# Scores of the second mixer's attention: two heads per token tile, the low K part in 64 rows each

## The chip, the cores and the metric

The kernel runs on one core of a Trainium2 chip, as one program launched once. The metric is the device time of that program in microseconds (us); the number that counts is the median of several runs.

## The reference, cut to what matters

Two layers are applied to two request groups of 512 tokens with the same weights. The change touches the second layer's mixer only: an attention with 16 heads of width 64 and rotary positions.

```python
def odd_mixer(x, w_in, w_out):
    q, k, v = jnp.split(x @ w_in, 3, axis=-1)
    q = rope(to_heads(q, DA_HEADS)) * DA_HEAD_DIM ** -0.5
    k = rope(to_heads(k, DA_HEADS))
    v = to_heads(v, DA_HEADS)
    res = [dilated_branch(q, k, v, w, d) for (w, d) in DA_BRANCHES]
    wts = jax.nn.softmax(jnp.stack([r[1] for r in res]), axis=0)
    o = jnp.einsum('gbht,gbhtd->bhtd', wts, jnp.stack([r[0] for r in res]).astype(jnp.float32))
    return from_heads(o.astype(x.dtype)) @ w_out
```

The three branches, mixed by their softmax denominators, are the same as one softmax over all 512 keys of the score plus the logarithm of the number of branches that hold the pair of positions. The kernel computes it in that form: `logc` holds minus that logarithm, and a huge number where no branch holds the pair.

## The kernel before

**Stages.** Layer 0 has its mixer and its mixture of experts, layer 1 the same; the attention of the second mixer runs from about 1405 to 1880 us of the profiled span. Each stage hands its result to the next through memory.

**Precision.** Matrix products are made of parts: a value is split in a high part, which the fast matmul format holds exactly, and the low rest. A product is hi x hi + lo x hi + hi x lo. Softmax weights and V are multiplied in full 32-bit, which the profile shows as two matmul records for each matmul.

**A unit.** `odd` works through 16 units, one for each pair of heads `p` (0 to 7) and request group `g`. `da_unit` returns the slots of a unit, and `weave` runs the slots with the steps of the next unit's projections (`steps_t`, and `steps_n` for V) spread between them. A unit has 8 blocks: head `e` of the pair (0 or 1) by token tile `t` (0 to 3), 128 queries each against 512 keys.

**A block.** `q_stack` puts Q hi of a head in its own 64 rows (rows 0 to 63 for head 0, 64 to 127 for head 1) and Q lo in the other 64. `k_stack` puts K hi in both halves of a tile `a`, and K lo in the head's own half of a tile `b`; `zero_halves` has filled the other half of `b` with zeros once. So one matmul of 128 rows, `q` by `a`, gives Q hi x K hi + Q lo x K hi, and a second one, `q` by `b`, adds Q hi x K lo. Both write the PSUM tile `s` (two buffers). VectorE then adds `logc` and takes the minimum in one pass (L825), ScalarE takes the exponential with its sum (L827), and VectorE takes the reciprocal and scales the row (L828, L829).

**Turning and closing.** `turn` transposes a block's weights in four 128x128 matmuls against `ident` (L837) into a PSUM tile `t` (two buffers), and one copy by ScalarE or VectorE takes it to `pt`. The transposes of a block follow the scores of the block two places later, as `attend` keeps two waiting. `close` multiplies the weights by V: eight matmuls, alternately for head 0 and head 1, each of 64 weight columns, so that the two heads stand in the two column halves of TensorE. The page shows these as `o<-pt,v 128*64`.

**Order.** Each engine executes its list in order. The list is made at build time by a scheduler, which may move instructions between slots where data allow it; several matmuls of `close` are thus put between the next unit's scores. All matmuls go through the helper at L134, so the tile names (`acc` projections, `s` scores, `t` transposes, `o` weights by V) tell them apart. K lo lies in spare parts of boxes named `mraw` and `mrawb`: `s<-mraw,qk` and `s<-mrawb,qk` are the K lo matmuls, `s<-qk` those with K hi. In the trace `128*128` is rows by weight columns of the array that a matmul takes.

Of the kernel before, what the change touches and what calls it, by code (L numbers as in the profile page):

```python
# [12 lines left out]
F32 = mybir.dt.float32  # L13
# [3 lines left out]
AF = mybir.ActivationFunctionType  # L17
OP = mybir.AluOpType
# [3 lines left out]
G, T, D = 2, 512, 1024  # L22
KT = D // 128
NT = T // 128
# [98 lines left out]
class Trunk:  # L123
# [207 lines left out]
    def turn(self, keep):  # L331
        while len(self.turns) > keep:
            turn, i, close = self.turns.popleft()
            turn(i)
            if close:
                self.late.append(close)
# [110 lines left out]
    def na_unit(self, g, p, qk, V, biases):  # L447
# [3 lines left out]
        def block(i):  # L451
            e, c2 = divmod(i, 2)
            q, (kh, kl), bias = qk["q"][e], qk["k"][e], biases[e]
            hv, lv = (x.rearrange("p (r c) -> p r c", c=64) for x in (kh, kl))
            S = self.ps.tile([128, 2, 256], F32, name="s", bufs=2)
            P = PS[i] = pb.tile([128, 2, 256], F32, name="p", bufs=3)
            st = pb.tile([128, 4, 2], F32, name="sm_st", bufs=4)
            for j in range(2):
                cb = 2 * c2 + j
                qs = q[:, 128 * cb:128 * cb + 128]  # L460
                b = slice(BAND[cb], BAND[cb] + 32)
                self.mm(S[:, j], qs, hv[:, :, b], True, False)
                self.mm(S[:, j], qs, lv[:, :, b], False, True)
            for j in range(2):
                nc.vector.tensor_tensor_reduce(P[:, j], S[:, j], bias[:, VAR[2 * c2 + j]], 1.0, 0.0,
                                               OP.add, OP.max, st[:, 0, j:j + 1])
            nc.vector.tensor_scalar(st[:, 1], st[:, 0], -1.0, None, op0=OP.mult)
            for j in range(2):
                nc.scalar.activation(P[:, j], P[:, j], AF.Exp, bias=st[:, 1, j:j + 1],
                                     accum_out=st[:, 2, j:j + 1])  # L470
            nc.vector.reciprocal(st[:, 3], st[:, 2])
            for j in range(2):
                nc.vector.tensor_scalar(P[:, j], P[:, j], st[:, 3, j:j + 1], None, op0=OP.mult)

# [60 lines left out]
    def ml_unit(self, g, h, qk, md, cols, V):  # L535
# [14 lines left out]
        def score(s):  # L550
            (qh, ql), (kh, kl), nm, nd = qk["q"], qk["k"], u["nm"], u["nd"]
            S = self.ps.tile([128, T], F32, name="s", bufs=2)
            c = slice(s * 128, (s + 1) * 128)
            self.mm(S, kh[:, c], qh, True, False)
            self.mm(S, kh[:, c], ql, False, False)
# [256 lines left out]
    def da_unit(self, g, p, qk, V):  # L812
        nc, pb = self.nc, self.pb
        PT, PS = [None, None], {}

        def block(i):
            e, t = divmod(i, 4)
            q, (kh, kl) = qk["q"][e], qk["k"][e]
            S = self.ps.tile([128, T], F32, name="s", bufs=2)
            c = slice(t * 128, (t + 1) * 128)  # L820
            self.mm(S, q[:, c], kh, True, False)
            self.mm(S, q[:, c], kl, False, True)
            P = PS[i] = pb.tile([128, T], F32, name="p", bufs=3)
            st = pb.tile([128, 3], F32, name="sm_st", bufs=4)
            nc.vector.tensor_tensor_reduce(P, S, self.logc[:, 384 - t * 128:384 - t * 128 + T], 1.0, 0.0,  # L825
                                           OP.add, OP.min, st[:, 0:1])
            nc.scalar.activation(P, P, AF.Exp, bias=st[:, 0:1], scale=-1.0, accum_out=st[:, 1:2])  # L827
            nc.vector.reciprocal(st[:, 2:3], st[:, 1:2])  # L828
            nc.vector.tensor_scalar(P, P, st[:, 2:3], None, op0=OP.mult)  # L829

        def turn(i):
            e, t = divmod(i, 4)
            if t == 0:
                PT[e] = pb.tile([128, 4, T], F32, name="pt", bufs=self.pt_bufs)
            tp = self.ps.tile([128, 4, 128], F32, name="t", bufs=2)
            for k in range(NT):
                nc.tensor.transpose(tp[:, k], PS[i][:, k * 128:(k + 1) * 128], self.ident)  # L837
            self.copy_any(PT[e][:, :, t * 128:(t + 1) * 128], tp)

        def close():  # L840
            o = self.ps.tile([128, T], F32, name="o", bufs=1)
            hc = (p % 2) * 128
            for k in range(NT):
                for e in range(2):
                    self.mm(o[64 * e:64 * e + 64], V[g, p // 2][:, k, hc + 64 * e:hc + 64 * e + 64], PT[e][:, k],
                            k == 0, k == NT - 1)
            self.y_store(g, p, o)

        return self.attend(block, turn, close, 8)

    def odd(self):
        nc, pb, a = self.nc, self.pb, self.a
# [43 lines left out]
        after = self.loaded, self.normed  # L896
        with self.tc.issue_after(after[0]), self.tc.issue_after(after[1]):
            self.W["q0"] += self.subhalf(a["wo"][1], 1)
        self.zero_halves()
        lnf, ap = [pb.tile([128, D], F32, name="v4", bufs=4) for _ in range(2)], a["lnf"][0]  # L900
        for i, t in enumerate(lnf):
            nc.sync.dma_start(t, bass.AP(tensor=ap.tensor, offset=ap.offset + i * D, ap=[[0, 128], [1, D]]))
# [51 lines left out]
        for i, (p, g) in enumerate(acts):  # L954
# [3 lines left out]
            else:  # L958
                self.open_out(1)
                rest = self.out_steps(1, 0)  # L960
                fill = rest[:8]
            self.weave(slots, fill)
        self.weave([partial(self.turn, 1), partial(self.turn, 0), self.drain], rest[8:])

    def router_weights(self, layer):
        nc, pd = self.nc, self.pd
# [524 lines left out]
```

## Time and profile before

| | |
|---|---|
| median of three runs | 2823.64 us (2819.38 to 2824.97) |
| profiled execution, its own time | 2821.07 us |
| its span, first to last instruction | 2819.3 us |
| mean granted TensorE clock | 0.978 of full speed |
| PE busy (matmul) | 2690.2 us, 95% |
| PEld busy (weight load, beside PE) | 2251.3 us, 80% |
| DVE (VectorE) / ACT (ScalarE) busy | 2254.6 us, 80% / 1836.7 us, 65% |

Busy time of PE counts matmul records, which overlap their neighbours, as results drain while the next matmul streams. What one matmul costs is therefore read from the distance between two starts, not from its length.

### The profile page before, as it was taken

How to read it: one execution, taken by the hardware profiler on the slowest of the kernel's cores; microseconds unless marked ns; L12 is line 12 of the kernel's file. 1: busy time of each engine (PE TensorE's matmuls, PEld its weight loads, DVE VectorE, ACT ScalarE, POOL GpSimd, SP SyncE). 2: the span in 40 equal slices, each digit the busy share in tenths (PEclk: the TensorE clock that was granted, in tenths of full speed). 3: DMA queues.
4: the chain of work that ended last, by engine and by line, in shares of the span. 5: the costliest groups of instructions: out<-in, count | busy, mean ns of one | idle time of the engine just before them, and what ended most of it. 6: DMA issues, size and time to landing. Idle time of an engine off the chain costs nothing.

```text
span 2819.3 us, 39964 instructions
## 1 busy us (share of the span) xinstructions
PE 2690.2 (95%) x14376; PEld 2251.3 (80%) x14376; DVE 2254.6 (80%) x3867; ACT 1836.7 (65%) x2737; POOL 180.6 (6%) x111
## 2 busy tenths in 40 slices
PE   8999999979999999999599999999799999999995
PEld 7888889868888888888477767679588888888873
DVE  4467687689989898989786776775899999999976
ACT  3555443367777878788466665752578778787864
POOL 0000000410000000000000000004100000000002
PEclk9999999989999999999799999999899999999997
DMA  6411236689899999995411010155898999999853
GB/s 209 152 62 55 77 106 221 226 355 391 352 409 368 393 416 361 415 392 184 142 68 38 29 50 24 56 191 223 347 389 352 408 368 392 418 359 417 352 228 138
DMA packets 118838, 714.33 MB, mean 253 GB/s; under 512 B 18509, under 2 KB 30285, under 8 KB 73311
## 3 DMA queue, kind: packets, MB, share of 16 engines
q1 hardware_dynamic: 108703, 671.40, 59.9%
q0 software_dynamic: 9936, 40.37, 5.1%
q8 instruction: 113, 1.85, 0.3%
q14 instruction: 86, 0.70, 0.1%
HBM read 657.16 MB, written 55.66 MB: 253 GB/s over the span
## 4 chain that ended last, share of the span: by engine, by line
PE 42%; DVE 5%; ACT 2%; DMA 2%; issue 1%; POOL 0%; SPq 0%; POOLq 0%; DVEq 0%; ACTq 0%
PE acc L134 18%; PE o L134 11%; PE s L134 10%; PE t L837 1%; PE t L147 1%; ACT rp L805 1%; DMA mrawp<-ws 1%; DVE rp L809 0%; DVE rp L807 0%; DVE rp L808 0%; DVE qk L408 0%; DVE p L825 0%; PE t L887 0%; ACT p L827 0%; DVE mrawb L144 0%
## 5 line engine op out<-in xcount | busy, mean ns | idle before, releaser
L144 DVE TENSOR_TENSOR mlo<-mraw,mhi 128x1024 fp32r<-128x1024 f32 (+1 forms) x486 | 527.6, 1139 | 41.0 <-ACT mhi L144 38.8
L144 ACT CAST mhi<-mraw 128x1024 fp32r<-128x1024 f32 (+1 forms) x486 | 450.3, 989 | 27.6 <-PE acc L134 12.8
L144 DVE TENSOR_TENSOR mlo<-mrawp,mhi 128x1024 fp32r<-128x1024 f32 (+1 forms) x282 | 316.7, 1173 | 29.0 <-ACT mhi L144 27.6
L144 DVE TENSOR_TENSOR mlo<-mrawb,mhi 128x1024 fp32r<-128x1024 f32 (+1 forms) x264 | 295.2, 1169 | 19.6 <-ACT mhi L144 18.2
L134 PE MATMUL s<-mhi,xeh 128*128 128x512 f32 (+1 forms) x768 | 290.2, 378 | 0.0
L134 PE MATMUL acc<-mhi,xeh 128*128 128x512 f32 (+1 forms) x768 | 288.1, 375 | 1.9 <-ACT mhi L144 1.9
L134 PE MATMUL acc<-mlo,xeh 128*128 128x512 f32 (+1 forms) x768 | 287.6, 374 | 1.2 <-DVE mlo L144 1.1
L144 ACT CAST mhi<-mrawp 128x1024 fp32r<-128x1024 f32 (+1 forms) x282 | 270.1, 1014 | 27.5 <-POOL xres L1079 10.2
L134 PE MATMUL acc<-mhi,xel 128*128 128x512 f32 (+1 forms) x768 | 287.5, 374 | 0.0
L134 PE MATMUL s<-mlo,xeh 128*128 128x512 f32 (+1 forms) x768 | 285.3, 372 | 0.0
L134 PE MATMUL s<-mhi,xel 128*128 128x512 f32 (+1 forms) x768 | 285.3, 371 | 0.0
L134 PE MATMUL o<-mhi,hh 128*128 128x512 f32 x704 | 279.8, 397 | 0.0
L134 PE MATMUL o<-mhi,hl 128*128 128x512 f32 x704 | 275.6, 391 | 0.0
L134 PE MATMUL o<-mlo,hh 128*128 128x512 f32 x704 | 275.1, 391 | 0.0
L144 ACT CAST mhi<-mrawb 128x1024 fp32r<-128x1024 f32 (+1 forms) x264 | 251.1, 1013 | 11.5 <-PE acc L134 4.4
L134 PE MATMUL acc<-mrawb,mraw 128*128 128x256 f32 (+1 forms) x1416 | 217.5, 309 | 13.3 <-ACT mrawb L144 10.9
L134 PEld LDWEIGHTS acc<-mrawb,mraw 128*128 128x128 f32 x1416 | 194.4, 193 | 28.1 <-ACT mrawb L144 11.1
L134 PE MATMUL acc<-mraw,mrawb 128*128 128x512 f32 x792 | 203.5, 399 | 0.0
L134 PE MATMUL acc<-xh,mrawb 128*128 128x512 f32 x528 | 186.1, 406 | 0.0
L134 PEld LDWEIGHTS acc<-mraw,mrawb 128*128 128x128 f32 x792 | 144.0, 188 | 31.2 <-issue 3.2
L134 PEld LDWEIGHTS acc<-mhi,xeh 128*128 128x128 f32 x768 | 145.9, 190 | 24.8 <-ACT mhi L144 3.2
L134 PEld LDWEIGHTS acc<-mlo,xeh 128*128 128x128 f32 x768 | 145.8, 190 | 23.8 <-DVE mlo L144 2.6
(337 smaller groups left out, 5152.8 us busy)
## 6 DMA issues: line engine op xcount, KB each, us to landing
mraw<-ws SPq DMA_DIRECT2D x150, 1536.0 KB
mrawp<-ws SPq DMA_DIRECT2D x90, 1536.0 KB
mrawb<-ws SPq DMA_DIRECT2D x82, 1536.0 KB
mraws<-ws SPq DMA_DIRECT2D x26, 1536.0 KB
mraw<-wo SPq DMA_DIRECT2D x24, 512.0 KB
mraw<-we SPq DMA_DIRECT2D x16, 512.0 KB
yd<-yst SPq DMA_DIRECT2D x32, 256.0 KB
mraw<-wn SPq DMA_DIRECT2D x12, 512.0 KB
```

Source lines behind the costliest of these rows:

```text
L134: return self.nc.tensor.matmul(out, lhsT, rhs, start=start, stop=stop, skip_group_check=True)
L144: return [self.nc.scalar.copy(hi, src), self.nc.vector.tensor_tensor(lo, src, hi, op=OP.subtract)]
L147: out = f(*args, **kw)
L805: nc.scalar.copy(r[32 * i:32 * i + 32], ps[32 * j:32 * j + 32])
L837: nc.tensor.transpose(tp[:, k], PS[i][:, k * 128:(k + 1) * 128], self.ident)
```

## The change

`da_unit` no longer goes through `attend`. A slot is now a token tile `t` with both heads: the K hi matmuls of head 0 and head 1, then their K lo matmuls, each of which takes only the 64 rows in which the head's Q hi and K lo lie (rows 0 to 63, rows 64 to 127). Then the two softmax chains. `turn` transposes both heads' blocks of one token tile, and one token tile is kept waiting in place of two blocks. There are 4 slots in place of 8, with the same projection steps between them, twice as many to a slot. The `p` buffers are 4 in place of 3. `odd` no longer zeroes the other halves (`zero_halves` is left out there); layer 0 is as before.

```diff
-        def block(i):
-            e, t = divmod(i, 4)
-            q, (kh, kl) = qk["q"][e], qk["k"][e]
-            S = self.ps.tile([128, T], F32, name="s", bufs=2)
+        def pair(t):
             c = slice(t * 128, (t + 1) * 128)
-            self.mm(S, q[:, c], kh, True, False)
-            self.mm(S, q[:, c], kl, False, True)
...
+            S = [self.ps.tile([128, T], F32, name="s", bufs=2) for _ in range(2)]
+            for e in range(2):
+                self.mm(S[e], qk["q"][e][:, c], qk["k"][e][0], True, False)
+            for e in range(2):
+                u = slice(64 * e, 64 * e + 64)
+                self.mm(S[e], qk["q"][e][u, c], qk["k"][e][1][u], False, True)
+            for e in range(2):
+                P = PS[t, e] = pb.tile([128, T], F32, name="p", bufs=4)
...
+        def turn(t):
+            for e in range(2):
+                if t == 0:
+                    PT[e] = pb.tile([128, 4, T], F32, name="pt", bufs=self.pt_bufs)
+                tp = self.ps.tile([128, 4, 128], F32, name="t", bufs=2)
+                for k in range(NT):
+                    nc.tensor.transpose(tp[:, k], PS[t, e][:, k * 128:(k + 1) * 128], self.ident)
+                self.copy_any(PT[e][:, :, t * 128:(t + 1) * 128], tp)
...
-        return self.attend(block, turn, close, 8)
+        def slot(t):
+            pair(t)
+            if self.late:
+                self.late.popleft()()
+            self.turns.append((turn, t, close if t == NT - 1 else None))
+            self.turn(1)
+
+        return [partial(slot, t) for t in range(NT)]
...
-        self.zero_halves()
+        self.kl_next = [0, 0]
```

How the change moves instructions is seen in the built lists. First the start of a unit on PE (TensorE), before: `o` rows are the previous unit's weights by V, `s` rows the new unit's scores, each score tile with its K hi row and then its K lo row (the one with `mraw`).

```order
L134 MATMUL o_14458<-pt_14181,v4_13336 64x512
L134 MATMUL s_14406<-qk_14398,qk_14343 128x512
L134 MATMUL s_14406<-mraw_12722,qk_14343 128x512
L134 MATMUL s_14428<-qk_14398,qk_14343 128x512
L134 MATMUL s_14428<-mraw_12722,qk_14343 128x512
L134 MATMUL o_14458<-pt_14321,v4_13336 64x512
L134 MATMUL o_14458<-pt_14181,v4_13336 64x512
L134 MATMUL s_14449<-qk_14398,qk_14343 128x512
L134 MATMUL s_14449<-mraw_12722,qk_14343 128x512
L134 MATMUL o_14458<-pt_14321,v4_13336 64x512
```

All three blocks are of head 0. The same place on PE of the changed kernel, where `s_14402` and `s_14445` are head 0 and `s_14403` and `s_14446` head 1:

```order
L134 MATMUL s_14402<-qk_14394,qk_14354 128x512
L134 MATMUL s_14402<-mraw_12722,qk_14354 128x512
L134 MATMUL o_14463<-pt_14193,v4_13348 64x512
L134 MATMUL o_14463<-pt_14186,v4_13348 64x512
L134 MATMUL s_14403<-qk_14398,qk_14357 128x512
L134 MATMUL s_14403<-mraw_12722,qk_14357 128x512
L134 MATMUL s_14445<-qk_14394,qk_14354 128x512
L134 MATMUL s_14445<-mraw_12722,qk_14354 128x512
L134 MATMUL o_14463<-pt_14193,v4_13348 64x512
L134 MATMUL o_14463<-pt_14186,v4_13348 64x512
L134 MATMUL s_14446<-qk_14398,qk_14357 128x512
L134 MATMUL s_14446<-mraw_12722,qk_14357 128x512
```

Here the scheduler has pulled the two heads apart again: no K lo matmul stands beside the other head's, and each is a 64-row matmul between matmuls of 128 rows. The second place is on PE inside the same unit, before: two blocks with their transposes.

```order
L134 MATMUL s_14483<-qk_14398,qk_14343 128x512
L134 MATMUL s_14483<-mraw_12722,qk_14343 128x512
L837 MATMUL t_14492<-ident_60,p_14431 128x128 x4
...
L134 MATMUL s_14519<-qk_14402,qk_14346 128x512
L134 MATMUL s_14519<-mraw_12722,qk_14346 128x512
L837 MATMUL t_14528<-ident_60,p_14452 128x128 x4
```

And in the changed kernel, where both heads' scores and then both heads' transposes stand together:

```order
L134 MATMUL s_14516<-qk_14394,qk_14354 128x512
L134 MATMUL s_14517<-qk_14398,qk_14357 128x512
L134 MATMUL s_14516<-mraw_12722,qk_14354 128x512
L134 MATMUL s_14517<-mraw_12722,qk_14357 128x512
L839 MATMUL t_14534<-ident_60,p_14451 128x128 x4
L839 MATMUL t_14540<-ident_60,p_14457 128x128 x4
```

Counted over the whole PE list, the 128 K lo matmuls of the changed kernel stand as 30 neighbouring pairs and 68 single ones. Between matmuls of different array shape (128 by 128, 64 weight columns, 64 rows and the few others) there are 150 places before and 323 after. Of the difference, 98 lead into a 64-row stretch and 98 out of one (31 of these into `o`, 30 into transposes, 37 into other matmuls of full shape). The rest are 23 fewer: 27 fewer from `s` and `acc` into `o`, 5 fewer from `o` into transposes, 7 more from `o` into `s`, 2 more from `o` into `acc`. The deeper of the two column halves in each stretch of `o` matmuls, summed over all stretches, is 79 matmuls before and 77 after. VectorE has four MEMSETs fewer; no other engine has a computing instruction more or fewer.

## Rows read from the trace of the kernel before

**Rows 1.** Busy time of each engine in the attention and its middle part.

```profile
core 0: us, PE busy (x) PEld busy (x) DVE busy (x) ACT busy (x) POOL busy (x), PEclk, DMA share, GB/s
1412.00:1875.00 463.00, 453.96 (x2480) 336.21 (x2479) 346.06 (x808) 301.00 (x597) 0.00 (x0) 1.00 0.15 52
1500.00:1840.00 340.00, 333.54 (x1758) 240.91 (x1757) 243.87 (x575) 219.94 (x437) 0.00 (x0) 1.00 0.12 42
```

**Rows 2.** Waits in 1410:1875: weight loads (PEld), then matmuls (PE); total, times, longest.

```profile
PEld o L134 <- issue: 30.6, 97, 0.9
PEld s L134 <- DVE sm_st L825: 12.8, 17, 1.3
PEld s L134 <- ACT qk L419: 11.6, 13, 1.2
...
PE s L134 <- ACT qk L419: 5.4, 10, 0.8
PE t L837 <- DVE sm_st L828: 1.9, 9, 0.3
```

**Rows 3.** PE timeline at a unit's start: start, length, instruction, idle before.

```profile
1537.32 0.50 PE L134 MATMUL s<-qk 128*128 128x512 f32 x1 [0.27 <-ACT qk L419]
1537.65 0.40 PE L134 MATMUL s<-mraw,qk 128*128 128x512 f32 x1
1537.88 0.39 PE L134 MATMUL s<-qk 128*128 128x512 f32 x1
1538.12 0.40 PE L134 MATMUL s<-mraw,qk 128*128 128x512 f32 x1
1538.44 1.08 PE L134 MATMUL o<-pt,v 128*64 128x512 f32 x4
1539.45 0.50 PE L134 MATMUL s<-qk 128*128 128x512 f32 x1
1539.79 0.39 PE L134 MATMUL s<-mraw,qk 128*128 128x512 f32 x1
```

**Rows 4.** PE timeline inside a unit, scores, transposes, projection.

```profile
1548.76 0.40 PE L134 MATMUL s<-mraw,qk 128*128 128x512 f32 x1
1549.00 0.60 PE L837 MATMUL t<-ident,p 128*128 128x128 f32 x4
1549.35 0.48 PE L134 MATMUL acc<-xh,mrawb 128*128 128x512 f32 x1
1549.67 0.39 PE L134 MATMUL acc<-xl,mrawb 128*128 128x512 f32 x1
```

**Rows 5.** PE timeline, transposes that follow weights by V.

```profile
1687.55 1.93 PE L134 MATMUL o<-pt,v 128*64 128x512 f32 x6
1689.41 0.66 PE L837 MATMUL t<-ident,p 128*128 128x128 f32 x4
```

**Rows 6.** PE timeline in layer 0: eight transposes of 64 rows between projections.

```profile
267.04 1.29 PE L134 MATMUL acc<-mrawb,mraw 128*128 128x512 f32 x5
268.26 0.71 PE L530 MATMUL t<-ident,mw 64*128 64x64 f32 x8
268.90 0.74 PE L134 MATMUL acc<-mrawb,xh 128*128 128x512 f32 x2
269.48 0.40 PE L134 MATMUL acc<-mrawb,xl 128*128 128x512 f32 x1
```

**Rows 7.** PE timeline near the end: a 32-bit matmul of one row, two records.

```profile
2737.36 0.39 PE L134 MATMUL s<-mlo,xeh 128*128 128x512 f32 x1
2737.59 0.39 PE L134 MATMUL s<-mhi,xel 128*128 128x512 f32 x1
2737.91 1.12 PE L134 MATMUL t<-mrawb,aff 1*128 1x512 f32 x2
```

**Rows 8.** PE timeline, one whole `close` after the last unit.

```profile
1876.26 3.65 PE L134 MATMUL o<-pt,v 128*64 128x512 f32 x16
```

**Rows 9.** DVE timeline ahead of the attention: a MEMSET of `zero_halves`, and what follows.

```profile
1343.97 0.48 DVE L395 MEMSET mrawb<- 64x512 f32 x1
1352.02 0.69 DVE L378 BATCH_NORM_STATS2 ln_st<-pt 128x6 f32<-128x512 f32 x1 [7.57 <-DMA pt<-y]
```

**Rows 10.** ACT timeline at the same unit's start as rows 3: K hi of head 0, then head 1.

```profile
1535.98 0.63 ACT L417 ACTIVATE qk<-rp 64x512 fp32r<-64x512 f32 x1 [1.47 <-DVE rp L809]
1536.63 0.63 ACT L419 ACTIVATE qk<-rp 64x512 fp32r<-64x512 f32 x1
1537.29 0.63 ACT L417 ACTIVATE qk<-rp 64x512 fp32r<-64x512 f32 x1
1537.94 0.63 ACT L419 ACTIVATE qk<-rp 64x512 fp32r<-64x512 f32 x1
```

More of the change, by code (lines that the diff above doesn't have):

```diff
@@ L814, in da_unit @@
         PT, PS = [None, None], {}
-        def block(i):
-            e, t = divmod(i, 4)
-            q, (kh, kl) = qk["q"][e], qk["k"][e]
-            S = self.ps.tile([128, T], F32, name="s", bufs=2)
+        def pair(t):
             c = slice(t * 128, (t + 1) * 128)
-            self.mm(S, q[:, c], kh, True, False)
-            self.mm(S, q[:, c], kl, False, True)
[L823 to L838, printed above, removed]
+            S = [self.ps.tile([128, T], F32, name="s", bufs=2) for _ in range(2)]
@@ new lines, in pair @@
+            for e in range(2):
[5 more added lines that the diff above has]
+                P = PS[t, e] = pb.tile([128, T], F32, name="p", bufs=4)
+                st = pb.tile([128, 3], F32, name="sm_st", bufs=4)
+                nc.vector.tensor_tensor_reduce(P, S[e], self.logc[:, 384 - t * 128:384 - t * 128 + T], 1.0, 0.0,
+                                               OP.add, OP.min, st[:, 0:1])
+                nc.scalar.activation(P, P, AF.Exp, bias=st[:, 0:1], scale=-1.0, accum_out=st[:, 1:2])
+                nc.vector.reciprocal(st[:, 2:3], st[:, 1:2])
+                nc.vector.tensor_scalar(P, P, st[:, 2:3], None, op0=OP.mult)
@@ L962, in odd @@
             self.weave(slots, fill)
-        self.weave([partial(self.turn, 1), partial(self.turn, 0), self.drain], rest[8:])
+        self.weave([partial(self.turn, 0), self.drain], rest[8:])
     def router_weights(self, layer):
```

## The prediction, as it was put on record

> **What bounds the kernel now.** I read the stretches first, then who waits for whom, then the timeline of TensorE. In the attention PE is busy 453.96 of 463.00 us and DVE and ACT 346.06 and 301.00 at a granted clock of 1.00 [rows 1]: the stage goes as fast as TensorE's stream of matmuls, and only 463.00 - 453.96 = 9.0 us are left in which PE has nothing in flight. The waits say the same. The longest entry is not a wait for an engine but "issue", 30.6 us in 97 pieces ahead of the weight loads of `o` [rows 2]. The reader should see in the timeline what that is. Two score matmuls follow each other by 0.23 us (1537.65, 1537.88). The first `o` after a score starts 0.32 us behind it (1538.12, 1538.44), though it waits for nothing. The score after the `o` matmuls starts at 1539.45, and its follower 0.34 us later [rows 3]. PE pays each time the shape of the array changes. So the question is how many matmul times the change removes and how many such changes it adds.
>
> **The price of a change of shape.** It has two parts. The array empties: 0.32 - 0.23 = 0.09 us. Then the first weights are loaded in the open, where otherwise they load behind the matmul before: 0.34 - 0.23 = 0.11 us for 128 weight columns of a product [rows 3]. For `o`, with half the weight columns, I take half of that, 0.05. For transposes it is 0.06: four take 0.66 behind `o` and 0.60 behind a score [rows 4, 5]. So 0.20 into a product, 0.14 into `o`, 0.15 into transposes. Transposes themselves cost no change of shape: they start 0.24 behind the score [rows 4].
>
> Does a 64-row matmul also count as another shape? No product of 64 rows is in the trace of before, but two near rows are. Eight transposes of 64 rows in layer 0: the five projections ahead start 0.23 apart, so the fifth starts at 267.04 + 1.29 - 0.39 = 267.94 and the next could at 268.17; the transposes start at 268.26, 0.09 later. Behind them the first two projections take 0.58 in place of 0.46, 0.12 for the load [rows 6]. And a matmul of one row of the array starts 0.32 behind a score, again 0.09, and its two records take 1.12 - 0.16 = 0.96, of which 2 x 0.43 are the product and 0.10 the load [rows 7]. (0.16 is what a record's modelled length stands over its stream: 0.39 at a distance of 0.23 [rows 3]. 0.43 is a record of a 32-bit product of 512 columns: 3.65 - 0.16 - 0.05 over the eight steps that 16 records in two halves make [rows 8].) Fewer rows cost as much as fewer columns. The Trainium skill's page "TensorEngine Tiling (Array Packing)", section "Tiling Modes", says that a change of tiling mode, not of the tile alone, drains the engine. It gives no price; here the drain is 0.09 us, and by the rule alone, without the load, the sum below would be some 20 us lower.
>
> **The change part by part.**
>
> K lo in 64 rows. A single one of 64 rows still streams 512 columns, 0.23 us, as before. Two neighbours, in different row halves and different PSUM tiles, can run at the same time. No row of before shows row halves side by side; the column halves do run so: 16 records of `close` take 3.65 us, half of what 16 in a row would at 0.43 [rows 8]. I take row halves as equal. The gain is one matmul for each neighbouring pair: 30 x 0.23 = 7.0 us, and nothing if they run in turn. It would be 64 x 0.23 = 15 us if all pairs were neighbours, but the list has only 30 together.
>
> Changes of shape. 98 into 64 rows at 0.20 = 19.6. Out: 31 x 0.14 = 4.3, 30 x 0.15 = 4.5, 37 x 0.20 = 7.4. The others: 7 x 0.20 + 2 x 0.20 - 27 x 0.14 - 5 x 0.15 = -2.7. Together +33.1 us. Bounds: if the load of K lo's weights hides, 98 x 0.11 = 10.8 less; a price below 0.09 is spoken against by both near rows.
>
> Weights by V. The column stretches are two matmuls less deep: 2 x 2 records x 0.43 = -1.7 us.
>
> Transposes in groups of two. They pay no load or drain behind scores, and the projection behind four of them starts 0.35 after their start and its follower 0.32 later, 0.67 for four transposes and one matmul, so four cost 0.44 [rows 4]. That is the same in a group of eight: 0.
>
> MEMSETs left out. Four of 0.48 us, the last at 1343.97, and DVE then sits idle 7.57 us for a transfer [rows 9]: 0. Without that gap they would cost 1.9.
>
> Softmax, copies and DMAs are as many as before; DVE and ACT have over 100 us of room in the stretch [rows 1], and the transfers are issued in the same places of the sequence, each released by work that PE paces.
>
> Waits. PE's stream grows by 33.1 - 7.0 - 1.7 = +24.4 us. Of the 9.0 us in which it idles, part goes, because slower PE work gives the chains through ACT and DVE more time: at most all 9.0. Against it, a block's weights are now wanted one token tile later rather than two blocks later, and the second half of them has the first one's chain ahead on DVE. I take -4, between -9 and +4.
>
> Sum: +24.4 - 4 = **+20 us** on the profiled 2821.07, so about 2841 for an execution like it. The profiled time is 2.6 us under the median of the runs, 2823.64; added to the median it gives **2843 us**. What comes behind the attention (output projection, router, experts) starts from its result and moves by as much.
>
> **Rivals.**
>
> *The halves do not overlap.* Then the 7.0 us do not come, and the sum is +27: 2850. The column halves speak against it [rows 8]; no row decides it for rows.
>
> *The second head's operands come too late.* A unit now needs both heads' Q and K at once. ACT writes head 1's K hi after head 0's: 1536.63 and 1537.94, 1.31 us later [rows 10], and PE already waits for that line 11.6 + 5.4 us in all [rows 2]. If PE idled 1.3 us at 15 unit starts, +20 more: 2863. Against it stands the new list: between the first score of head 0 and that of head 1 stand a K lo matmul and two `o`, 0.23 + 0.20 + 0.87 + 0.14 and the change back of 0.20, or 1.6 us of work. It decides only where the scheduler leaves less than 1.3 there.
>
> *A change to 64 rows is free for products.* Then pairs give -7.0, the columns -1.7, and a K lo counts as a full matmul: the places into and out of `o` change by +8 at about 0.17, +1.4. Sum -7.3: 2816, faster. For it: no row shows a fast-format product of 64 rows. Against: a fast-format product follows or precedes in both near rows, and both pay [rows 6, 7]. It decides below 0.05 us per change: 8.7 gained over 173 more places. The Trainium skill's page "TensorE: Matmul & The Clock Gate", Part 3 ("The mechanism"), speaks for this side: it has small matmuls in different row groups start about 4 ns apart and counts no cost of going in and out. By it alone the time would be this rival's.
>
> **How the numbers follow.** The forecast has 0.66, no overlap 0.13, late operands 0.09, free changes 0.07, and 0.05 is left for a sum near zero (loads hidden, all idle time gone: 24.4 - 10.8 - 9.0 = +4.6, or 2828). A measurement of this kernel can tell about 0.2%, 5.6 us, from no change. So slower 0.66 + 0.13 + 0.09 = 0.88, same 0.05, faster 0.07. The range goes from 2828, the lower bound just worked out, to 24.4 + 7.0 + 4 = +35, or 2858: it holds the forecast and the case without overlap, 0.79.
>
> **What the profile after would show.** K lo rows as `64*128`. Each 64-row matmul starts about 0.32 behind the one ahead, and the next of full shape 0.43 behind it. In a pair the two K lo matmuls start within some ns of each other; 0.23 apart would mean no overlap. "issue" waits of weight loads of `s`, `acc` and `t` grow by over 100 pieces. The attention takes some 20 us more, DVE and ACT are busy as long as before, and every stretch behind it is as long as before. I am wrong if the starts round a 64-row matmul stay 0.23 apart, or if PE's waits for `qk` and `sm_st` move by more than the 9 us that I allow.

## The result, and the profile after

The changed kernel takes **2851.24 us** (median of 4 runs, 2846.58 to 2853.43); the kernel before took 2822.24 beside it (4 runs, 2819.38 to 2824.97). The ratio is 1.0102, with a 95% interval from 1.0089 to 1.0114: 29.0 us slower. The forecast was 2843, with a range from 2828 to 2858. The direction is the one forecast and the size 8 us short.

The profiled execution of the changed kernel is the fastest of its four, 2846.58 us with a span of 2844.8, and stands 25.5 us above that of before. Its busy time, share of the span and count of instructions of each engine:

```profile
PE 2717.2 (96%) x14376; PEld 2248.5 (79%) x14376; DVE 2250.2 (79%) x3863; ACT 1834.4 (64%) x2737; POOL 180.0 (6%) x111
```

Where the 25.5 us went is seen by cutting both spans at the same events: the first score matmul of the attention, the start of the last single matmul of its weights by V, the first MAX of the second layer's top-k, the first matmul and the last up product of its experts.

| Stage | before, us | after, us | difference |
|---|---|---|---|
| up to the first score of the attention | 1402.75 | 1401.57 | -1.2 |
| attention, to its last `o` matmul | 476.6 | 499.1 | **+22.6** |
| output projection and router, to top-k | 101.5 | 107.8 | **+6.3** |
| top-k to the first expert matmul | 19.8 | 19.8 | 0 |
| experts, to the last up product | 751.7 | 748.6 | -3.1 |
| to the end | 67.0 | 67.9 | +0.9 |

The two bold rows make 28.9 us; the whole difference is 25.5 between these two executions and 29.0 between the medians. The -3.1 of the experts is the clock that TensorE was granted: late in that stage the execution before has 6.8 us at 0.50 of full speed (2740.5 to 2747.3), which is 3.4 us less than full speed gives, and the execution after has no such stretch there. Whether the change has a part in that is not shown.

**The attention.** Busy time of each engine between the first score and the end of the last `o`, before (the first line names the columns, and they hold for every row of this kind below: stretch, its length, busy time and count of each engine, granted clock, share of the DMA engines, GB/s):

```profile
core 0: us, PE busy (x) PEld busy (x) DVE busy (x) ACT busy (x) POOL busy (x), PEclk, DMA share, GB/s
1402.75:1879.91 477.16, 468.08 (x2558) 346.40 (x2558) 357.65 (x831) 312.42 (x617) 0.00 (x0) 1.00 0.15 52
```

and after:

```profile
1401.57:1901.28 499.71, 491.91 (x2549) 341.35 (x2549) 353.66 (x828) 309.86 (x616) 0.00 (x0) 0.99 0.14 49
```

TensorE still has something in flight nearly all the time. Its busy time is 491.91 - 468.08 = 23.8 us longer, and the time in which it has nothing is 1.3 us shorter (477.16 - 468.08 = 9.1, now 499.71 - 491.91 = 7.8). So the stage did not get a new wait: the stream of matmuls itself takes longer, with no more of them. VectorE and ScalarE do no more than before.

Not all of the 23.8 us is the shape of the array. At the start of the attention the clock is granted at 0.50, the 1.2 GHz level. Before, that lasts 3.14 us:

```profile
1402.75:1405.89 3.14, 3.10 (x9) 2.19 (x10) 2.47 (x5) 3.04 (x5) 0.00 (x0) 0.50 0.00 0
```

and after, 10.37 us, in all of which PE is busy:

```profile
1401.57:1411.94 10.37, 10.37 (x26) 6.04 (x26) 7.21 (x19) 7.83 (x14) 0.00 (x0) 0.50 0.00 1
```

In both the clock had fallen in the idle time ahead of the stage (8.04 us in one piece). The added 7.23 us at half speed are 3.6 us less than full speed gives, so some 20.2 of the 23.8 us are left for the stream itself. The forecast has no such term. The timeline of PE shows the rest, in one place of the changed kernel (start, length, instruction):

```profile
1588.54 0.63 PE L134 MATMUL s<-qk 128*128 128x512 f32 x2
1589.10 0.49 PE L134 MATMUL s<-mrawb,qk 64*128 64x512 f32 x2
1589.52 1.09 PE L839 MATMUL t<-ident,p 128*128 128x128 f32 x8
...
1599.17 0.50 PE L134 MATMUL s<-qk 128*128 128x512 f32 x1 [0.25 <-ACT qk L419]
1599.61 0.50 PE L134 MATMUL s<-mraw,qk 64*128 64x512 f32 x1
```

The two K lo matmuls of 64 rows stand in one row of 0.49 us; the single one ten microseconds later has 0.50. Two take the time of one: the row halves do work side by side (in all 30 pairs the second starts 3 to 4 ns behind the first). But from the first score to the transposes it is 1589.52 - 1588.54 = 0.98 us, and four full matmuls at the 0.23 of [rows 3] make 0.93. The pair saved a matmul and going in and out of its shape took it back: the pair starts 0.33 behind the second score in place of 0.23, and the transposes 0.42 behind the pair. The weight loads of the same place show why:

```profile
1588.32 0.41 PEld L134 LDWEIGHTS s<-qk 128*128 128x128 f32 x2
1589.10 0.19 PEld L134 LDWEIGHTS s<-mrawb,qk 64*128 64x128 f32 x2 [0.36 <-issue]
```

The weights of the scores begin to load at 1588.32, 0.22 ahead of their first matmul at 1588.54. Those of the pair begin at 1589.10, together with the matmuls that use them.

The waits of the weight loads in 1410:1905 (in total, times, longest), to be read against [rows 2]:

```profile
PEld s L134 <- issue: 31.5, 103, 0.8
PEld o L134 <- issue: 28.0, 102, 0.4
PEld s L134 <- ACT qk L419: 17.6, 19, 1.8
PEld t L839 <- issue: 14.6, 39, 0.8
PEld acc L134 <- issue: 14.6, 34, 0.8
```

"issue" ahead of `s` is new, with 103 pieces, and for `t` and `acc` it has 39 and 34 pieces where before had 17 and 9. All 103 of the first and all 34 of `acc` stand where the shape changes: there the load does not begin while the matmul ahead runs. `o` is much as before (97 pieces, 30.6).

**Behind the attention.** Here the forecast had nothing, and 6.3 us came. PE's timeline in the second part of the output projection (in brackets: idle time before, and what ended it):

```profile
1913.12 1.19 PE L134 MATMUL acc<-mrawb,mraw 128*128 128x256 f32 x6 [3.24 <-ACT mraw L144]
1914.97 2.31 PE L134 MATMUL acc<-mrawb,mraw 128*128 128x256 f32 x7 [0.66 <-DVE mraw L144]
```

Before, the same place of the program reads

```profile
1887.99 11.36 PE L134 MATMUL acc<-mrawb,mraw 128*128 128x256 f32 x92 [1.46 <-ACT mraw L144]
```

Two idle pieces, 3.90 us together, stand in place of one of 1.46, and what comes behind them runs slowly. The windows show it:

```profile
1910.70:1913.10 2.40, 0.00 (x0) 0.00 (x0) 1.29 (x2) 1.81 (x3) 0.00 (x0) 1.00 1.02 341
1913.10:1916.00 2.90, 2.20 (x9) 1.61 (x9) 1.78 (x5) 0.00 (x0) 0.00 (x0) 0.60 0.91 323
1916.00:1918.00 2.00, 1.94 (x9) 1.94 (x10) 0.81 (x4) 0.00 (x0) 0.00 (x0) 0.50 1.00 381
1918.00:1920.00 2.00, 2.00 (x11) 2.00 (x11) 0.34 (x1) 0.13 (x1) 0.00 (x0) 0.50 1.07 430
1920.00:1922.00 2.00, 2.00 (x17) 2.00 (x16) 0.18 (x2) 1.27 (x3) 0.00 (x0) 0.87 1.02 432
1922.00:1930.00 8.00, 8.00 (x70) 8.00 (x70) 5.10 (x10) 0.35 (x1) 0.00 (x0) 1.00 0.74 239
```

While PE stands idle the clock is still granted in full; behind the piece of 3.24 us it falls to 0.50, and it is back at full speed, 2.4 GHz, only after 1920. PE starts 9 + 11 matmuls in the 4 us from 1916, and 70 in the 8 us from 1922. From 1913.10 to 1922.00 it is granted 2.90 x 0.40 + 4.00 x 0.50 + 2.00 x 0.13 = 3.4 us less than full speed, some of it while PE idles again. With the 2.4 us of added idle time that is at most 5.8 of the 6.3.

What PE waits for is ScalarE's split of the last loaded attention rows, and those come from SP's queue (start, length, instruction). After:

```profile
1903.16 0.41 SPq L159 DMA_DIRECT2D lnp<-lnm  x1
1906.66 1.53 SPq L205 DMA_DIRECT2D mraw<-woo  x2
1909.10 0.33 SPq L1024 DMA_DIRECT2D mraw<-yd  x1
```

and before:

```profile
1884.60 0.32 SPq L1015 DMA_DIRECT2D mraw<-yd  x1
1884.97 0.43 SPq L159 DMA_DIRECT2D lnp<-lnm  x1
1885.61 1.52 SPq L205 DMA_DIRECT2D mraw<-woo  x2
```

The single load `mraw<-yd` came ahead of the layer-norm parameters `lnp` and of two loads of projection weights; now it stands behind all three. Counted from the start of the last `close` (16 matmul records of `o`), it is issued 11.5 us later (1909.10 - 1897.63) in place of 8.3 (1884.60 - 1876.26). No line of the diff writes this load; the scheduler put it elsewhere. One line of the diff, not in the extract of the section on the change, does act close by: the last eight steps of the output projection's first part are spread over two slots in place of three.

```diff
-        self.weave([partial(self.turn, 1), partial(self.turn, 0), self.drain], rest[8:])
+        self.weave([partial(self.turn, 0), self.drain], rest[8:])
```

Which line moved the load is not shown. That one alone does not: run 6 below keeps it, and there the load stands ahead of `lnp` and the two `woo` again.

### The profile page after: what moved, and what is told of

Read it like the earlier page. It is cut to its first block, busy times and chain, and to the rows that moved or that the text cites. A ratio compares the mean times of both kernels' runs of the same rounds, so it can differ in the third digit from the quotient of the medians.

```text
span 2844.8 us, 39958 instructions
## 1 busy us (share of the span) xinstructions
PE 2717.2 (96%) x14376; PEld 2248.5 (79%) x14376; DVE 2250.2 (79%) x3863; ACT 1834.4 (64%) x2737; POOL 180.0 (6%) x111
## 4 chain that ended last, share of the span: by engine, by line
PE 42%; DVE 5%; ACT 4%; DMA 2%; issue 1%; SPq 0%; POOLq 0%; DVEq 0%; ACTq 0%
PE acc L134 17%; PE s L134 11%; PE o L134 10%; ACT rp L805 2%; PE t L839 1%; PE t L147 1%; DMA mrawp<-ws 1%; ACT p L829 0%; DVE rp L809 0%; DVE rp L807 0%; PE t L896 0%; DVE rp L808 0%; DVE mlo L144 0%; DVE ln_st L378 0%; ACT qk L407 0%
## 5 line engine op out<-in xcount | busy, mean ns | idle before, releaser
L144 DVE TENSOR_TENSOR mlo<-mrawp,mhi 128x1024 fp32r<-128x1024 f32 (+1 forms) x282 | 316.8, 1175 | 28.6 <-ACT mhi L144 27.2
L134 PEld LDWEIGHTS acc<-mhi,xeh 128*128 128x128 f32 x768 | 144.9, 189 | 24.4 <-ACT mhi L144 2.9
```

What stands on the lines that cost most here:

```text
L134: return self.nc.tensor.matmul(out, lhsT, rhs, start=start, stop=stop, skip_group_check=True)
L144: return [self.nc.scalar.copy(hi, src), self.nc.vector.tensor_tensor(lo, src, hi, op=OP.subtract)]
```

## The experiments

Theory: each place at which the array changes shape costs TensorE about 0.2 us, 30 pairs give back 0.23 each, and the rest of the loss is the order of transfers behind the attention. The rivals were that the pairing or its waits cost the time whatever the shape, and that shape changes with 64 rows are cheap. "Places" are those at which two neighbours on PE differ in array shape: 150 before, 323 after.

**1. All 128 rows in K lo, the rest of the change kept.** The pairs, the groups of two and the new order stay; `zero_halves` is back, and K lo runs over the full array (158 places).

```diff
             for e in range(2):
-                u = slice(64 * e, 64 * e + 64)
-                self.mm(S[e], qk["q"][e][u, c], qk["k"][e][1][u], False, True)
+                self.mm(S[e], qk["q"][e][:, c], qk["k"][e][1], False, True)
...
-        self.kl_next = [0, 0]
+        self.zero_halves()
```

> The changed order (token tile by token tile, both heads, transposes in groups of two) with K lo as a matmul of all 128 rows, zeros in the other half, as in the kernel before. Theory 1 (changes of array shape cost the time): the list has 158 places where the shape changes, before 150 and the changed kernel 323, so the attention takes within 3 us of before. Its transfer list at the output projection is that of the changed kernel, in which the last loads of attention results stand later, so what that costs stays: 4 to 6 us. Time 2822 + 5 = 2827. Rival (the second head's operands come too late, and the new order as such costs): the attention stays 20 us over before, time 2845 to 2851.

Measured: 2828.86 us (2825.33 to 2831.80), ratio 1.0024 [1.0014, 1.0034]. The attention of this kernel:

```profile
1403.27:1880.68 477.41, 468.04 (x2549) 346.38 (x2549) 352.93 (x828) 308.41 (x615) 0.00 (x0) 1.00 0.15 51
```

PE is busy 468.04 us against 468.08 before: everything in the change but the 64 rows costs the attention nothing. The clock at its start is that of before too, though this kernel issues its first matmuls in the order of the changed one:

```profile
1403.27:1406.72 3.45, 3.36 (x9) 2.31 (x10) 2.27 (x6) 3.35 (x5) 0.00 (x0) 0.50 0.00 0
```

Most of the 7.4 us that stay are behind it: from the last `o` to the top-k it is 5.7 us longer than before (the experts' stage is 1.0 longer), and its SP queue has the order of after (`mraw<-yd` behind `lnp` and two `woo`), with one PE wait in 1870:1985 that stands out:

```profile
PE acc L134 <- ACT mraw L144: 4.0, 1, 4.0
```

So the two losses come apart: about 24 us of the attention are the 64 rows (20.4 in the stream, and 3.5 by the longer stretch at 0.50), and about 6 us the order of the transfers, which comes without any 64-row matmul too.

**2. 64 rows in the kernel before, nothing else.** One head per block as before, K lo in 64 rows, 124 of the 128 single (381 places).

```diff
             c = slice(t * 128, (t + 1) * 128)
+            u = slice(64 * e, 64 * e + 64)
             self.mm(S, q[:, c], kh, True, False)
-            self.mm(S, q[:, c], kl, False, True)
+            self.mm(S, q[u, c], kl[u], False, True)
```

> The order of before, block by block, with K lo as a matmul of 64 rows. 381 places of changing shape against 150, and only 2 neighbouring pairs. Theory 1: 231 places at about 0.18 us each, +41 us in the attention; the transfer list at its end is that of before, so nothing there. Time 2863. Rival (the new order costs, 64 rows cost nothing): 2822.

Measured: 2858.97 us (2853.89 to 2863.76), ratio 1.0139 [1.0122, 1.0156]. Its PE timeline, as the price without any pairing:

```profile
1548.66 0.49 PE L134 MATMUL s<-mraw,qk 64*128 64x512 f32 x1
1549.08 0.50 PE L134 MATMUL s<-qk 128*128 128x512 f32 x1
1549.51 0.49 PE L134 MATMUL s<-mraw,qk 64*128 64x512 f32 x1
```

From one K lo to the next it is 0.85 us, where [rows 3] have 1538.12 - 1537.65 = 0.47. Two changes of shape cost 0.38, or 0.19 each. Over the stretch PE is busy

```profile
1402.11:1915.47 513.36, 507.76 (x2558) 345.25 (x2558) 360.82 (x831) 312.67 (x617) 0.00 (x0) 0.99 0.14 48
```

39.7 us more for 231 more places. The clock at the start takes 1.8 of them (6.7 us at 0.50 in place of 3.1), which leaves (39.7 - 1.8) / 231 = 0.164 each. The two pairs that came about by themselves give nothing back: their K lo matmuls start 0.33 and 0.34 us apart, one after the other. By their place in the list both of a pair are of head 0, so they take the same 64 rows. Its idle time falls from 9.1 to 5.6. Behind the attention this kernel is 0.6 us shorter than before, and its transfers stand there in the order of before. This run alone rules out that 64 rows are free.

**3. All pairs but one side by side.** The changed kernel, with the K lo matmuls held behind both K hi (63 neighbouring pairs, 286 places).

```diff
             for e in range(2):
-                self.mm(S[e], qk["q"][e][:, c], qk["k"][e][0], True, False)
-            for e in range(2):
-                u = slice(64 * e, 64 * e + 64)
-                self.mm(S[e], qk["q"][e][u, c], qk["k"][e][1][u], False, True)
+                hi = self.mm(S[e], qk["q"][e][:, c], qk["k"][e][0], True, False)
+            with self.tc.issue_after(hi.ins):
+                for e in range(2):
+                    u = slice(64 * e, 64 * e + 64)
+                    self.mm(S[e], qk["q"][e][u, c], qk["k"][e][1][u], False, True)
```

> The changed kernel with each token tile's K lo matmuls held behind both K hi matmuls, so that 63 of 64 pairs are neighbours; 286 places of changing shape. Theory 1: against before 136 places at 0.18 = +24, less 63 pairs at 0.23 = -14, so +10 in the attention, some us of waiting for the second head, and the later loads behind it, 5. Time 2837 to 2842, under the changed kernel. Rival (late operands of the second head cost): PE now has to wait for both heads at each unit's start, 15 times 1.3 us, so over the changed kernel, 2855 or more.

Measured: 2841.25 us (2840.00 to 2845.22), ratio 1.0075 [1.0058, 1.0092], in the expected range.

```profile
1402.17:1891.57 489.40, 479.03 (x2549) 334.82 (x2549) 353.76 (x828) 308.51 (x615) 0.00 (x0) 0.99 0.15 50
```

PE is busy 11.0 us longer than in run 1, for 128 more places, 63 pairs, columns two matmuls deeper and 1.5 us by the clock at the start (6.4 us at 0.50 in place of 3.45): (11.0 - 1.5 + 63 x 0.233 - 2 x 0.86) / 128, about 0.18 us for a place. The idle time is 10.4. Behind the attention it takes 7.2 us more than before, and the late load stands behind the others as in the changed kernel. A unit's start shows what the order costs in waits:

```profile
1543.33 0.50 PE L134 MATMUL s<-qk 128*128 128x512 f32 x1 [0.94 <-ACT qk L419]
1543.77 1.08 PE L134 MATMUL o<-pt,v 128*64 128x512 f32 x4
1544.77 0.51 PE L134 MATMUL s<-qk 128*128 128x512 f32 x1
1545.21 0.51 PE L134 MATMUL s<-mraw,qk 64*128 64x512 f32 x2
```

PE waits for K hi, as in [rows 3], and the scheduler fills the gap between the heads with `o`, of a third shape, so that the second score pays once more. Even with 63 of the 64 pairs together the change stays slower than before.

**4. The late load put forward, first attempt.** The changed kernel, with the order in the output projection's second part written so that the late load comes behind one weight load.

```diff
         if part:
-            W.append(self.subgrains(w[1], grains))
-        for g in range(G):
-            y_load(g, ks[-1], 1)
+            W.append(self.subgrains(w[1], grains[:1]))
+            y_load(0, ks[-1], 1)
+            W[1] += self.subgrains(w[1], grains[1:])
+            y_load(1, ks[-1], 1)
...
```

> The changed kernel with the last attention results of the first request group loaded ahead of two of the output projection's weight loads; the attention itself is as in the changed kernel. Theory 1 says that 4 to 6 us of the 29 come from the place of these loads in the transfer queue: time 2846, and PE's idle of 3.2 us at the start of the output projection's second part goes back to about 1.5. Rival (that difference is chance from run to run): 2851, as the changed kernel.

Measured: 2854.46 us (2853.96 to 2857.30), ratio 1.0119 [1.0103, 1.0136], a miss. The edit also acts on the first layer's output projection, and there it costs: PE idles 4.52 us in one piece where before it idles 0.88, and the first score of the attention comes at 1409.8, 7.1 us later than in the kernel before. In the second layer the stretch behind the attention is 3.3 us over before in place of 6.3. The run mixes two effects and decides nothing; run 7 does it cleanly.

**5. Weights by V in one piece.** From the kernel before, without the change: the eight matmuls (16 records) of a `close` are held behind the score ahead and the next score behind them, so that they stay together (102 places; the deeper column halves sum to 65 in place of 79).

```diff
-            self.mm(S, q[:, c], kh, True, False)
-            self.mm(S, q[:, c], kl, False, True)
+            with self.tc.issue_after(self.last_o) if self.last_o else nullcontext():
+                self.mm(S, q[:, c], kh, True, False)
+                self.last_s = self.mm(S, q[:, c], kl, False, True).ins
...
-            for k in range(NT):
-                for e in range(2):
-                    self.mm(o[64 * e:64 * e + 64], V[g, p // 2][:, k, hc + 64 * e:hc + 64 * e + 64], PT[e][:, k],
-                            k == 0, k == NT - 1)
+            with self.tc.issue_after(self.last_s):
+                for k in range(NT):
+                    for e in range(2):
+                        i = self.mm(o[64 * e:64 * e + 64], V[g, p // 2][:, k, hc + 64 * e:hc + 64 * e + 64],
+                                    PT[e][:, k], k == 0, k == NT - 1)
+            self.last_o = i.ins
...
```

(In a slot the late `close` is now called ahead of the block.)

> The kernel before, with K lo in 128 rows and block by block, where the eight matmuls of weights by V are held together: the next unit's scores issue ahead of all eight or behind them. 102 places of changing shape against 150, and the column stretches are 65 matmuls deep in place of 79. Theory 1: 48 places at 0.17 = -8 and 14 x 0.86 = -12, so -20 us in the attention, some of it lost to waits that the interleaved matmuls covered: time 2802 to 2810. Rival (interleaving is what hides the wait for the next unit's operands, and changes of shape are cheap): 2822 or over.

Measured: **2802.30 us** (2800.18 to 2804.79) against 2822.08, ratio 0.9930 [0.9917, 0.9944]: faster than both kernels. The same kind of place as [rows 3]:

```profile
1535.76 0.50 PE L134 MATMUL s<-qk 128*128 128x512 f32 x1 [0.26 <-ACT qk L419]
...
1536.88 3.65 PE L134 MATMUL o<-pt,v 128*64 128x512 f32 x16
```

and the stretch:

```profile
1403.11:1862.71 459.60, 449.18 (x2558) 346.50 (x2558) 357.92 (x831) 309.98 (x617) 0.00 (x0) 1.00 0.16 55
```

PE is busy 18.9 us less with the same matmuls. By the prediction's prices it is 14 x 0.86 = 12.0 for columns that no longer run alone and 48 places at 0.14 to 0.20, 6.7 to 9.6: 18.7 to 21.6. The idle time grows to 10.4. Of the 20 us, 17.6 are in the attention and 1.8 behind it.

**6. Runs 3 and 5 together.** The changed kernel with forced pairs and whole `close` (220 places, 63 pairs, column halves 64 deep).

```diff
...
+            with self.tc.issue_after(self.last_o) if self.last_o else nullcontext():
+                for e in range(2):
+                    hi = self.mm(S[e], qk["q"][e][:, c], qk["k"][e][0], True, False)
+                with self.tc.issue_after(hi.ins):
+                    for e in range(2):
+                        u = slice(64 * e, 64 * e + 64)
+                        i = self.mm(S[e], qk["q"][e][u, c], qk["k"][e][1][u], False, True)
+            self.last_s = i.ins
...
+            with self.tc.issue_after(self.last_s):
...
```

> The changed kernel with its K lo matmuls as neighbours (63 of 64 pairs) and with the weights by V held together: 220 places of changing shape. It is the change with nothing cut apart by the scheduler. Theory 1: against the run with the weights by V held together alone, 118 places more at 0.18 = +21, less 63 pairs at 0.23 = -14.5, so 6 or 7 us slower than that run: the change loses even so. Time 2809 to 2817. Rival (the change loses only because the scheduler cuts the pairs and the weights by V apart): equal to that run or faster, 2795 to 2802.

Measured: 2814.79 us (2813.87 to 2816.12), ratio 0.9971 [0.9959, 0.9983], in the range expected, and 12.5 us above run 5, which has whole `close` too and no 64-row matmul. Its best place:

```profile
1525.78 0.63 PE L134 MATMUL s<-qk 128*128 128x512 f32 x2
1526.33 0.49 PE L134 MATMUL s<-mrawb,qk 64*128 64x512 f32 x2
1526.76 1.09 PE L842 MATMUL t<-ident,p 128*128 128x128 f32 x8
```

It is the 0.98 us of the changed kernel once more. A pair between full matmuls gains nothing, however often it is brought about.

```profile
1404.15:1875.73 471.58, 460.82 (x2549) 332.43 (x2549) 355.15 (x830) 307.20 (x617) 0.00 (x0) 0.99 0.16 53
```

Against run 5 PE is busy 11.6 us longer, idle time nearly the same (10.8): 63 pairs save 14.7 and one depth less 0.9, so 118 more places cost 27.2, of which 1.8 are the clock at the start (6.9 us at 0.50 in place of 3.3): about 0.22 each. That is above the 0.16 to 0.18 of the other runs; why is not settled. Behind the attention it takes only 0.3 us more than before, with the late load early in SP's queue.

**7. The transfers in the order of before.** The changed kernel; in the second layer alone the late load stands behind one weight load again, and the two other weight loads, `lnp`, the router's weights and the first expert loads are held behind it.

```diff
-        if part:
-            W.append(self.subgrains(w[1], grains))
-        for g in range(G):
-            y_load(g, ks[-1], 1)
+        if part and layer:
+            W.append(self.subgrains(w[1], grains[:1]))
+            y_load(0, ks[-1], 1)
+            with self.tc.issue_after(self.y_last):
+                W[1] += self.subgrains(w[1], grains[1:])
+            y_load(1, ks[-1], 1)
...
-        lnp = self.bcast(pd, "lnp", a["lnm"][layer], [2, D])
+        with self.tc.issue_after(self.y_last) if layer else nullcontext():
+            lnp = self.bcast(pd, "lnp", a["lnm"][layer], [2, D])
...
```

> The changed kernel with the last loads of attention results ahead of the layer norm's and the output projection's remaining loads, for the second layer alone, about as the list of before has them; the attention is that of the changed kernel. Theory 1: the output projection takes 101 to 103 us again in place of 107.8, so 2845 to 2847. Rival (the 6 us there have another cause, as a later result of the last unit): 107 us, 2851.

Measured: 2844.17 us (2842.11 to 2845.39), ratio 1.0074 [1.0059, 1.0090], 0.8 us under the range expected. SP's queue and PE in this kernel:

```profile
1909.22 0.32 SPq L1024 DMA_DIRECT2D mraw<-yd  x1
1909.59 0.43 SPq L159 DMA_DIRECT2D lnp<-lnm  x1
1910.43 1.53 SPq L205 DMA_DIRECT2D mraw<-woo  x2
```

```profile
1914.10 3.55 PE L134 MATMUL acc<-mrawb,mraw 128*128 128x256 f32 x27 [0.28 <-DVE mraw L1056]
```

```profile
1911.00:1921.00 10.00, 9.70 (x77) 9.15 (x76) 6.27 (x14) 2.48 (x4) 0.00 (x0) 1.00 0.98 365
```

The load is issued 9.2 us after the start of the last `close` (which is at 1900.05), PE idles 0.28 us, the clock is granted in full, and from the last `o` matmul to the top-k it takes 0.35 us more than before in place of 6.3. The median falls by 7.1 us from that of the changed kernel, and the attention stays at +22.9, with 10.5 us at 0.50 at its start. With the transfers as before, the change costs 22.1 us: the 20 of the forecast and 2 more.

## Why the prediction was right, and where it failed

**The price of a change of shape** was right in kind, drain and load both, and a little high. Forecast 0.14 to 0.20, by kind, 33.1 / 173 = 0.191 on the mean; measured over whole stretches, less what the clock at the start takes, 0.16 (run 2, against before), 0.17 (after against run 1: (23.9 - 3.5 + 7.0) / 165) and 0.18 (run 3 against run 1). The Trainium skill's page "TensorEngine Tiling (Array Packing)", section "Tiling Modes", has a change of mode drain the engine, and the runs agree: 0.33 in place of 0.23 on the way in. The same runs show that the drain is about half of it. By the drain alone 165 places would be 15 us, and after against run 1 shows 27.4. (The prediction puts its sum without the load some 20 us lower; by its own prices it is 33.1 - 173 x 0.09 = 17.5.)

**Row halves side by side** was right: the pairs start 3 to 4 ns apart, and the rival without overlap falls. Neighbours in the same half do not overlap (0.33 and 0.34 apart in run 2). The Trainium skill's page "TensorE: Matmul & The Clock Gate", Part 3 ("The mechanism"), has about 4 ns, which the trace agrees with. As a rule for the time it would have led to the wrong side, since the way in and out is not in it: run 2 and after both rule out the rival of free changes.

**PE's stream** was forecast at +24.4, and PE's busy time grew by 23.8. That the two lie so close is luck. 3.6 of the 23.8 are the clock at the start of the attention, which the prediction put at nothing: it took a granted clock of 1.00 from [rows 1], and that stretch begins at 1412.00, behind the 3.14 us at 0.50 of before. At full speed the stream grew by 20.2, 4.2 less than forecast: with the 7.0 of the pairs and the 1.7 of the columns that is 28.9 for 173 places, 0.167 each. That the columns gained 1.7 and the groups of two and the MEMSETs nothing fits run 1, where 8 more places and the 1.7 come to a busy time as before.

**Waits** were put at -4, between -9 and +4. They gave -1.3. The mechanism (slower PE work covers the chains) shows better in run 2, with -3.5. In the changed kernel the weight loads do wait longer for `qk`, 17.6 us against 11.6, but most of it is covered by matmuls still running: PE's own waits for that line are 6.4 us in 10 pieces between the first score and the last `o`, against 6.1 in 11 before. The rival of late operands, 20 us more, falls.

**"What comes behind the attention ... moves by as much"** is the step that failed most, and with it "the transfers are issued in the same places of the sequence". I had compared PE's list and not SP's. One load went behind three others, and that cost 6.3 us, 2.4 of added idle time and most of the rest the clock. Run 1 shows the loss with no 64-row matmul at all (+5.7), run 2 shows none with more 64-row matmuls and the old order (-0.6), and run 7 takes it out by order alone. The other runs agree: run 3 has the late order and +7.2, runs 5 and 6 the early one and -1.8 and +0.3. The row that gave the warning was before's: PE already idled 1.46 us there for the same load, so that nothing covered a delay.

So the time fell into the range with errors that partly cancel. Of the 8.2 us by which the forecast was short, 6.3 are the order of the transfers, 2.7 the waits and 3.6 the clock at the start, less 4.2 for the stream; that these sum to 8.4 and not 8.2 lies between profiled executions and medians. What stays open: why the clock stays at 0.50 longer where the first scores have 64-row matmuls among them, and which line moved the late load. The experts' stage follows its clock in every run: it is 2.9 and 3.1 shorter than before's in runs 2 and 5, which lack the 6.8 us at 0.50 as the changed kernel does, and 1.0 longer in run 1, which has them.

## What to carry to other kernels

Before putting a smaller matmul into part of the array, count the places at which its neighbours have another shape: here a visit cost 0.38 us and a side-by-side partner gave back 0.23, so a small matmul pays only in a run of its own kind, and keeping existing small ones together (run 5, 20 us less) was worth more than making new ones. Look at the granted clock at a stage's start as well as over the whole of it: a mean of 0.99 here hid 3.6 us. An edit in one stage also moves what other queues issue near it: compare the order on the DMA-issuing engine too, above all where the profile of before shows the next stage waiting already for a transfer. A short stall of TensorE costs more than its length where the clock falls behind it: here 2.4 us of added idle time, and up to 3.4 by the clock.

## What was not expected of the hardware

- Behind one idle piece of 3.24 us TensorE's granted clock fell from 1.00 to 0.50, until about 1920. With 0.28 us of idle time in the same place (run 7) and with 1.46 (before, where 1888.00 to 1900.00 is granted in full) it stayed at 1.00.
- At the start of the attention the clock stays at 0.50 for 6.4 to 10.5 us in the six kernels with 64-row matmuls, and for 3.1 to 3.5 in the three without, though in the changed kernel PE is busy for all of its 10.37 us. Run 1 has the same order of matmuls there and 3.45 us. The runs do not show why.
- A full array's transposes behind a 64-row pair start 0.42 behind it, as late as a full product or a column-half `o` does (0.42 to 0.43): the way out takes the same time whichever of them comes next.
